# First phase of one diffusion-transformer layer on one core: the context's transfers as one piece behind the first two tiles, and a tile's products always behind the next tile's modulation

## The chip, the cores and the metric

The kernel runs on one core of a Trainium2 chip, with TensorE (PE, weight loads shown apart as PEld), VectorE (DVE), ScalarE (ACT), GpSimd (POOL) and SyncE (SP, which here issues nearly all transfers). The metric is the device time of one execution in microseconds; lower is better.

## The reference, cut to what matters

One layer over 256 latent tokens `x` and 256 context tokens `ctx`, D_MODEL = 2048, all in float32:

```python
mod   = (jax.nn.silu(c)     @ w_mod[l] + b_mod[l])[:, None, :]
sa, ca, ga, sm, cm, gm = jnp.split(mod, 6, axis=-1)
mod_c = jax.nn.silu(c_ctx)  @ w_mod[l] + b_mod[l]
...
h_c = modulate(x_ctx, norm_attn_w[l], sa_c, ca_c)     # rmsnorm(x) * (1 + scale) + shift
p_c_kv = h_c @ w_in[l][:, K_OFF:P_OFF]                # keys and values of the context
h = modulate(x, norm_attn_w[l], sa, ca)
p = h @ w_in[l]                                       # queries, keys, values, pool input, gates
...
mix = token_mixer(...)                                # attention + pooling, gated
x = x + ga * mix
x = x + gm * sq_relu_mlp(modulate(x, norm_mlp_w[l], sm, cm), w_ff1[l], w_ff2[l])
```

The change lies in the first phase: the shift `sa` and scale `ca` of both token sets, the hidden states `h` and `h_c` made from them, and the first half (512 columns, "group 0") of the queries of `x` and of the keys of `x` and `ctx`.

## The kernel before, in words

**Tiles.** D_MODEL is cut into 16 tiles `f` of 128 features (`KT = 16`). For each tile the kernel loads four 512 KB pieces of the modulation weight (`w_m`, f, i = 0..3), and PE multiplies them with the two conditioning vectors into a PSUM bank (`mod_tile`; 32 recorded matmuls a tile, rows `mod<-raw,cv`). ACT copies the result out (`rows`), PE turns it into columns (`modT`), ACT copies these (`col`), DVE adds bias and norm weight (`col`, L378 and L379). Then `hidden(f, t, ...)` makes the tile's modulated tokens, for x (t = 0, `hL`) and for the context (t = 1, `hC`): DVE `hw`, ACT the high part, DVE the low part. Every float32 product is made of three matmuls of parts (`mm3`): high by high, high by low, low by high.

**Products.** The weights of queries and keys come in pieces of two tiles (`w_q` and `w_k`, group 0, pair j for the tiles 2j and 2j+1). `load_next` issues the transfer and then splits the piece: ACT casts the high part (L224) and DVE subtracts the low part (L225). For each tile PE then runs 18 matmuls of 512 columns: two token tiles times three matmuls for each of "kx" (keys of x), "q" (queries) and "kc" (keys of the context). The high part's matmul of a token tile comes first, the low part's second.

**Order of transfers.** `plan` writes out the stream of pieces by hand, and SP issues them in this order; a piece waits in SP's queue until its buffer is free. The plain pieces (`raw`) share 5 buffers: the four `w_m` pieces of an even tile, and each `w_k` and `w_q` piece. The pieces of an odd tile have four buffers of their own. Context tokens (`cT`, four transfers of 512 KB) stand between `w_m` pieces of tiles 2 and 3. Pieces j = 0, 1, 3, 4, .. 7 stand behind the odd tile f = 2j+1, and piece 2 behind tile 6.

**Order on PE.** It is fixed by hand in this phase (`ordered_pe`). In the loop over `f`, `PACE[f]` steps of a list of products (`order`, a step is three matmuls) are put around the turn of tile f: half before `mod_columns`, half behind. The list lags: at odd tile f it works on a pair whose pieces were split a tile or more before, and the last 12 steps (pair 7) stand behind the loop. Context squares are summed at tiles 2 and 3, the context's scale `rms` is made at tile 4, and the context's hidden states of tiles 0 to 6 follow at tiles 4, 5 and 6 (`context`).

**Order on ACT and DVE at an odd tile.** Behind the tile's `mod` matmuls ACT has `rows`, the cast of the keys' piece (`first`), then `col` and the cast of the queries' piece (`whi`), and DVE the matching subtractions. The lines that set this are

```python
for w in ("w_k", "w_q"):
    held[w, j] = wchunk(w, 0, j, ahead=FIRST_AHEAD if j < 7 else 1)
steps(PACE[f] // 2)
cols[f] = mod_columns(f, rows)
```

After the phase come values, attention beside pooling and gates, the output projection and the MLP; nothing of these is edited.

Of the kernel before, what the change touches and what calls it, by code (L numbers as in the profile page):

```python
# [19 lines left out]
KT = D // P  # L20
# [28 lines left out]
def layer(ctx: ExitStack, tc, a, out):  # L49
# [21 lines left out]
    def bank(name):  # L71
        return psum.tile([P, 512], F32, tag="ps", name=name)

    def work(name, shape=None, dt=F32):
        return pool.tile(shape or [P, 512], dt, tag="w2", name=name, bufs=9)

    def s16(name, shape, dt=F32):
        return pool.tile(shape, dt, tag="s16", name=name, bufs=7)
# [4 lines left out]
    def small(name, n):  # L83
        return pool.tile([P, 16], F32, tag="sm", name=name, bufs=12)[:, 0:n]
# [14 lines left out]
    def tick():  # L99
        for w in waiting:  # L100
            w[0] -= 1
        while waiting:
            due = [w for w in waiting if w[0] <= 0]
            if not due:
                break
            waiting.remove(due[0])
            due[0][1]()
# [10 lines left out]
    def chain(*gens):  # L118
        for g in gens:
            yield from g  # L120
# [5 lines left out]
    def plan(name, *idx, rate=0.0):  # L126
        stream.append(((name,) + idx, rate))
# [3 lines left out]
    for f in range(KT):  # L131
        for i in range(4):
            plan("w_m", f, i)
            if f in (2, 3) and i % 2 == 1:
                plan("cT", 2 * f - 4 + i // 2)
            if (f, i) == (9, 0):
                plan("prq")
        j = 2 if f == 6 else -1 if f == 5 or f % 2 == 0 else f // 2
        if j >= 0:
            plan("w_k", 0, j)  # L140
            plan("w_q", 0, j)
    for n, g, rate in (("w_v", 0, 1.5), ("w_q", 1, 1.0), ("w_k", 1, 1.5), ("w_v", 1, 1.5)):
        for ch in range(8):
            plan(n, g, ch, rate=rate)
# [27 lines left out]
    FIRST_AHEAD = 3  # L172
# [22 lines left out]
    def load_next():  # L195
        key, rate = stream[len(loaded)]
        src = a[key[0]]
        for i in key[1:]:
            src = src[i]
        if key[0] == "prq":  # L200
            nc.sync.dma_start(prq, src)
            loaded.append((key, None, None))
            return
        if key[0] in ("cT", "x"):
            dst = cT[:, 4 * key[1]:4 * key[1] + 4, :] if key[0] == "cT" else x1_tile()[:, key[1], key[2] * 512:key[2] * 512 + 512]
            nc.sync.dma_start(dst, src)
            loaded.append((key, None, None))
            return
        n = src.shape[-1]
        if key[0] == "w_m":  # L210
            raw = mod_raw(*key[1:])
            sp.dma_start(raw, src)
            loaded.append((key, raw, raw))
            return
        raw = raw_chunk(src, n)
        if key[:2] == ("w_k", 0):
            if not first:
                first.append(s16("first", [P, 4, 1024], F32R))
            i = 2 * (key[2] % 2)
            hi, lo = first[0][:, i, :], first[0][:, i + 1, :]  # L220
        else:
            hi = pool.tile([P, n], F32R, tag="whi", name="whi", bufs=3)
            lo = pool.tile([P, n], F32R, tag="wlo", name="wlo", bufs=3)
        act.copy(hi, raw)  # L224
        vec.tensor_sub(lo, raw, hi.bitcast(F32))  # L225
        loaded.append((key, hi, lo))
        credit[0] += rate
        credit_rate[0] = rate
        while credit[0] >= 1.0:
            credit[0] -= 1.0  # L230
            if late[0] is not None:
                next(late[0], None)

    def wchunk(*key, ahead=AHEAD):
        while len(loaded) < min(done[0] + 1 + ahead, len(stream)) or loaded[done[0]][1] is None:
            if loaded and done[0] < len(loaded) and loaded[done[0]][1] is None:
                done[0] += 1
                continue
            load_next()
        got, hi, lo = loaded[done[0]]  # L240
        assert got == key, (got, key)
        loaded[done[0]] = None
        done[0] += 1
        tick()
        return hi, lo
# [27 lines left out]
    cT = s16("cT", [P, KT, T])  # L273
# [3 lines left out]
    def pr(name):  # L277
        lo, hi = PRM[name]
        return prm[:, lo:hi]
# [89 lines left out]
    def mod_columns(f, rows):  # L369

        pt = bank("modT")
        for a in range(2):
            pe.matmul(pt[:, 2 * a:2 * a + 2], rows[:, a * P:a * P + P], quads, start=a == 0, stop=a == 1,
                      skip_group_check=True)
        col = small("col", 4)
        act.copy(col, pt[:, 0:4])
        c3 = col.rearrange("p (a c) -> p a c", a=2)
        vec.tensor_add(c3, c3, bias2[:, :, f:f + 1].broadcast_to([P, 2, 2]))  # L378
        vec.tensor_scalar(c3[:, 0, :], c3[:, 0, :], pr("nw")[:, f:f + 1], None, ALU.mult)  # L379
        return c3  # L380

    def hidden(f, t, c3):

        src, h = ((xT, hL), (cT, hC))[t]
        u = work("hw", [P, T])
        ht, k8 = h[f // 8], f % 8
        bias = c3[:, 1, t:t + 1]
        vec.scalar_tensor_tensor(u, src[:, f, :], c3[:, 0, t:t + 1], rms[t], ALU.mult, ALU.mult)
        act.activation(ht[:, 0, k8, :], u, AF.Identity, bias=bias)
        vec.scalar_tensor_tensor(ht[:, 1, k8, :], u, bias, ht[:, 0, k8, :].bitcast(F32), ALU.add, ALU.subtract)  # L390

    def tokens(nt):
        return [(hL, 0), (hL, 1), (hC, 0), (hC, 1)][:nt]

    def xmm(banks, toks, k, hi, lo, sl, first, last):
        for ps, (h, t) in zip(banks, toks):
            mm3(ps, tok(h, k, 0, t), tok(h, k, 1, t), hi[:, sl], lo[:, sl], first, last)
# [72 lines left out]
    fb = {}  # L470
    held = {}

    def pair_steps(n, j):

        w = "w_q" if n == "q" else "w_k"
        if w not in fb:
            fb[w] = [bank(f"{w}_{t}") for t in range(4 if n != "q" else 2)]
        hi, lo = held[w, j]
        for kk in range(2):
            k = 2 * j + kk  # L480
            for t in range(2):
                t4 = t + (2 if n == "kc" else 0)
                xmm([fb[w][t4]], [tokens(4)[t4]], k, hi, lo, slice(kk * 512, kk * 512 + 512), k == 0, k == KT - 1)
                yield

    def steps(n):
        for _ in range(n):
            next(side, None)

    order = [("kx", 0), ("q", 0), ("kx", 1), ("q", 1), ("kc", 0), ("kc", 1), ("kx", 2), ("q", 2), ("kc", 2)]  # L490
    for j in range(3, 7):
        order += [("kx", j), ("q", j), ("kc", j)]
    side = chain(*(pair_steps(*o) for o in order))
    PACE = (0, 0, 4, 4, 6, 6, 8, 8) + (6,) * 8

    cols = {}
    total = []

    def context_squares(i):

        sq = [work("sq") for _ in range(2)]
        for h in range(2):
            act.activation(sq[h], cT[:, 4 * i + 2 * h:4 * i + 2 * h + 2, :].rearrange("p a t -> p (a t)"), AF.Square)
        vec.tensor_add(sq[0], sq[0], sq[1])
        if total:
            vec.tensor_add(total[0], total[0], sq[0])
        else:
            total.append(sq[0])


    context = {4: (0, 1), 5: (2, 3, 4), 6: (5, 6)}
    ordered_pe[0] = True
    sb = bank("ssq")
    for i in range(4):
# [2 lines left out]
    for f in range(KT):  # L517
        if f % 2 == 0:
            ps = bank("mod")
        rows = mod_tile(f, ps)  # L520
        if f == 4:
            sq = total[0]
            vec.tensor_add(sq[:, 0:T], sq[:, 0:T], sq[:, T:2 * T])
            sb = bank("ssq")
            pe.matmul(sb[:, 0:T], mean, sq[:, 0:T], start=True, stop=True)
            rms.append(rsq(sb[:, 0:T], T, P / D, "rms"))
        j = 2 if f == 6 else -1 if f == 5 or f % 2 == 0 else f // 2
        if j >= 0:
            for w in ("w_k", "w_q"):
                held[w, j] = wchunk(w, 0, j, ahead=FIRST_AHEAD if j < 7 else 1)  # L530
        steps(PACE[f] // 2)
        cols[f] = mod_columns(f, rows)
        steps(PACE[f] - PACE[f] // 2)
        hidden(f, 0, cols[f])
        for k in context.get(f, (f,) if f > 6 else ()):
            hidden(k, 1, cols[k])
        if f in (2, 3):
            for i in range(2):
                context_squares(2 * f - 4 + i)
        if f == 10:  # L540
            tables()
    lasts = [pair_steps(n, 7) for n in ("kx", "q", "kc")]
    for _ in range(2):
        for g in lasts:
            next(g)
            next(g)
    ordered_pe[0] = False
    kb, qb = fb["w_k"], fb["w_q"]
    qT = s8("qT", [P, NH, T])
# [558 lines left out]
```

## Time and profile before

| | us |
|---|---|
| median of 3 runs (1491.62 to 1492.20) | 1492.11 |
| the profiled execution: its own time | 1492.22 |
| its span, first to last instruction | 1490.40 |
| around the span (time less span) | 1.82 |
| first phase: first `mod` matmul to the first matmul of the values | 12.63 to 143.35 |
| `mod` matmuls of tile 5 start | 54.60 |
| `mod` matmuls of tile 15 start | 128.66 |

The profiled execution lies 0.11 us above the median. In a timeline row the first two numbers are start and length in us, `xN` the recorded instructions merged into the row, and a bracket at its end is the idle time of the engine before it and what ended it. A row of stages gives, after the two limits, its length and then the busy time and the count of each engine, the granted PE clock (1.00 is full), the busy share of the DMA engines and GB/s.

### The profile page before, as it was taken

The numbers are of one execution on the slowest core, as the hardware profiler recorded it, in microseconds if no ns is written. First come the engines' busy times: TensorE is split into PE (matmuls) and PEld (weight loads), VectorE is DVE, ScalarE is ACT, GpSimd is POOL, SyncE is SP. The second block draws the span as 40 slices with busy tenths as digits, with TensorE's granted clock in tenths as the row PEclk, the third lists the DMA queues.
The fourth block names the chain that finished last, engine by engine and source line by source line (L and its number), as shares of the span: only waits on it lengthen the run. The fifth ranks groups of instructions, "written<-read, shape, count | busy, mean of one in ns | idle before, by whom it ended". The sixth has DMA issues, their size and how long they took to land.

```text
span 1490.4 us, 19996 instructions
## 1 busy us (share of the span) xinstructions
PE 1450.0 (97%) x7578; PEld 1201.2 (81%) x7578; DVE 992.8 (67%) x1220; ACT 694.3 (47%) x956; POOL 121.2 (8%) x120
## 2 busy tenths in 40 slices
PE   5899999999899999999989999999999999999998
PEld 3567887778788888888879888888888888888887
DVE  3555988859887676767675765666666555555675
ACT  4435344555554444445444654545445453544532
POOL 0000101101410000000000100100000000000260
PEclk8999999999999999999999999999999999999999
DMA  9898696556678887897746777677776656666664
GB/s 380 314 371 309 206 313 215 156 162 205 212 247 269 267 269 260 263 311 257 230 147 201 239 238 238 223 234 237 242 235 215 192 190 193 188 192 190 186 197 140
DMA packets 97440, 347.85 MB, mean 233 GB/s; under 512 B 11072, under 2 KB 11712, under 8 KB 97344
## 3 DMA queue, kind: packets, MB, share of 16 engines
q1 hardware_dynamic: 96768, 345.50, 70.5%
q8 instruction: 59, 0.97, 0.3%
q0 software_dynamic: 576, 1.08, 0.2%
q14 instruction: 37, 0.30, 0.1%
HBM read 344.44 MB, written 2.10 MB: 233 GB/s over the span
## 4 chain that ended last, share of the span: by engine, by line
PE 90%; DMA 4%; DVE 3%; ACT 1%; issue 1%; SPq 1%; POOL 0%; DVEq 0%; POOLq 0%; ACTq 0%
PE f L957 14%; PE f L418 8%; PE f L419 8%; PE f L421 8%; PE f L960 7%; PE pg L419 4%; PE pg L418 4%; PE pg L421 4%; DMA raw<-in_w_m_dram 2%; PE wo L419 2%; PE wo L418 2%; PE wo L421 2%; PE pyy L418 2%; PE pyy L419 2%; PE pyy L421 2%; PE w_k L67 2%
## 5 line engine op out<-in xcount | busy, mean ns | idle before, releaser
L225 DVE TENSOR_TENSOR wlo<-raw,whi 128x1024 fp32r<-128x1024 f32 x443 | 547.6, 1238 | 355.5 <-ACT whi L224 334.3
L224 ACT CAST whi<-raw 128x1024 fp32r<-128x1024 f32 x443 | 463.8, 1048 | 577.0 <-PE f L419 184.8
L957 PE MATMUL f<-h,whi 128*128 128x512 f32 x896 | 224.2, 392 | 0.0
L418 PE MATMUL f<-whi,act 128*128 128x512 f32 x512 | 199.3, 389 | 0.0
L419 PE MATMUL f<-whi,act 128*128 128x512 f32 x512 | 199.3, 389 | 0.0
L957 PEld LDWEIGHTS f<-h,whi 128*128 128x128 f32 x896 | 161.7, 189 | 29.3
L598 DVE SCALAR_TENSOR_TENSOR macc<-raw,sil,macc 128x1024 f32<-128x1024 f32 x128 | 167.8, 1311 | 2.3 <-DMA macc<-in_b_ga_dram 1.3
L421 PE MATMUL f<-wlo,act 128*128 128x512 f32 x512 | 136.8, 389 | 0.0
L960 PEld LDWEIGHTS f<-h,wlo 128*128 128x128 f32 x896 | 122.2, 190 | 8.7
L960 PE MATMUL f<-h,wlo 128*128 128x256 f32 x896 | 124.9, 282 | 0.0
L421 PEld LDWEIGHTS f<-wlo,act 128*128 128x128 f32 x512 | 96.1, 188 | 19.9
L418 PEld LDWEIGHTS f<-whi,act 128*128 128x128 f32 x512 | 96.2, 188 | 19.8
L419 PEld LDWEIGHTS f<-whi,act 128*128 128x128 f32 x512 | 96.1, 188 | 19.8
L418 PE MATMUL pg<-whi,hL 128*128 128x512 f32 x256 | 100.7, 394 | 0.0
L419 PE MATMUL pg<-whi,hL 128*128 128x512 f32 x256 | 99.7, 389 | 0.0
L968 POOL TENSOR_TENSOR rsq<-relu 128x512 f32<-128x512 f32 x28 | 29.1, 1041 | 537.2 <-ACT relu L967 516.9
L421 PE MATMUL pg<-wlo,hL 128*128 128x512 f32 x256 | 68.5, 389 | 0.0
L419 PEld LDWEIGHTS pg<-whi,hL 128*128 128x128 f32 x256 | 48.1, 188 | 10.2 <-issue 0.2
L418 PEld LDWEIGHTS pg<-whi,hL 128*128 128x128 f32 x256 | 48.1, 188 | 10.2 <-ACT whi L224 0.2
L421 PEld LDWEIGHTS pg<-wlo,hL 128*128 128x128 f32 x256 | 48.1, 188 | 10.0
L67 PE MATMUL mod<-raw,cv 128*32 128x256 f32 x512 | 36.5, 401 | 15.6 <-DMA raw<-in_w_m_dram 15.6
L418 PE MATMUL wo<-whi,mix 128*128 128x512 f32 x128 | 49.9, 390 | 0.0
(254 smaller groups left out, 2116.9 us busy)
## 6 DMA issues: line engine op xcount, KB each, us to landing
raw<-in_w_ff_dram SPq DMA_DIRECT2D x240, 512.0 KB, 4.3
raw<-in_w_m_dram SPq DMA_DIRECT2D x64, 512.0 KB, 8.3
raw<-in_w_ga_dram SPq DMA_DIRECT2D x32, 512.0 KB, 4.5
raw<-in_w_cm_dram SPq DMA_DIRECT2D x32, 512.0 KB, 4.5
raw<-in_w_gb_in_dram SPq DMA_DIRECT2D x32, 512.0 KB, 4.5
raw<-in_w_ga_in_dram SPq DMA_DIRECT2D x32, 512.0 KB, 4.7
raw<-in_w_sm_dram SPq DMA_DIRECT2D x32, 512.0 KB, 5.0
raw<-in_w_o_dram SPq DMA_DIRECT2D x32, 512.0 KB, 4.5
```

The costliest lines, as they stand in the source:

```text
L67: return (lambda *a, **k: pin(emit(*a, **k))) if self.flag[0] else emit
L224: act.copy(hi, raw)
L225: vec.tensor_sub(lo, raw, hi.bitcast(F32))
L418: pe.matmul(banks[t], tok(h, k, 0, tt), wt, start=k == 0, stop=False)
L419: pe.matmul(banks[t], tok(h, k, 1, tt), wt, start=False, stop=False)
L421: pe.matmul(banks[t], tok(h, k, 0, tt), wt, start=False, stop=k == 2 * nk - 1)
L598: pin(vec.scalar_tensor_tensor(acc, raw, sil[:, 0, k:k + 1], acc, ALU.mult, ALU.add))
L957: pe.matmul(ps, hi[:, kk * P:kk * P + P], both(h2, k), start=k == 0, stop=False)
L960: pe.matmul(ps[:, T:2 * T], lo[:, kk * P:kk * P + P], act_slice(h2, k, 0), start=False, stop=k == KT - 1)
L968: gp.tensor_mul(sq, r, r)
```

## The change

The plan now puts the `w_k` and `w_q` piece j behind each odd tile f = 2j+1, piece 2 too, and the four context transfers behind the first such pair. The list of steps and `PACE` are gone: `products(n, k)` runs one tile's six matmuls of one kind. At tile 1, products "kx" and "q" of tiles 0 and 1 follow, then the squares, sum and scale of the whole context, and the context's hidden states of tiles 0 and 1. At tile 2, "kc" of tiles 0 and 1. From tile 3 on, behind the `mod` matmuls of tile f: "kx" of tile f-1, the turn and both hidden states of tile f, "q" and "kc" of tile f-1. Tile 15's own 18 matmuls stand behind the loop.

```diff
@@ plan
-            if f in (2, 3) and i % 2 == 1:
-                plan("cT", 2 * f - 4 + i // 2)
...
-        j = 2 if f == 6 else -1 if f == 5 or f % 2 == 0 else f // 2
-        if j >= 0:
-            plan("w_k", 0, j)
-            plan("w_q", 0, j)
+        if f % 2 == 1:
+            plan("w_k", 0, f // 2)
+            plan("w_q", 0, f // 2)
+        if f == 1:
+            for i in range(4):
+                plan("cT", i)
@@ products
-    order = [("kx", 0), ("q", 0), ("kx", 1), ("q", 1), ("kc", 0), ("kc", 1), ("kx", 2), ("q", 2), ("kc", 2)]
...
-    PACE = (0, 0, 4, 4, 6, 6, 8, 8) + (6,) * 8
+    def products(n, k):
+        w = "w_q" if n == "q" else "w_k"
...
+        hi, lo = held[w, k // 2]
+        c = (k % 2) * 512
+        for t in range(2):
+            t4 = t + (2 if n == "kc" else 0)
+            xmm([fb[w][t4]], [tokens(4)[t4]], k, hi, lo, slice(c, c + 512), k == 0, k == KT - 1)
+    def modulate(f, rows):
+        cols[f] = mod_columns(f, rows)
+        hidden(f, 0, cols[f])
+        if f > 1:
+            hidden(f, 1, cols[f])
@@ loop over f, behind rows = mod_tile(f, ps)
-        if f == 4:
+        if f < 3:
+            modulate(f, rows)
+        if f % 2 == 1:
+            for w in ("w_k", "w_q"):
+                held[w, f // 2] = wchunk(w, 0, f // 2, ahead=5 if f == 1 else FIRST_AHEAD if f < KT - 1 else 1)
+        if f == 1:
+            for k in range(2):
+                products("kx", k)
+                products("q", k)
+            for i in range(4):
+                context_squares(i)
             sq = total[0]
...
+            for k in range(2):
+                hidden(k, 1, cols[k])
+        elif f == 2:
+            products("kc", 0)
+            products("kc", 1)
+        elif f > 2:
+            products("kx", f - 1)
+            modulate(f, rows)
+            products("q", f - 1)
+            products("kc", f - 1)
...
+    for n in ("kx", "q", "kc"):
+        products(n, KT - 1)
```

On SP, before, from the first modulation pieces on (`xN` merges equal rows): one context transfer after every second `w_m` piece of tiles 2 and 3.

```order
L212 DMA raw<-in_w_m_dram 128x1024 x8
L115 DMA raw<-in_w_k_dram 128x1024
L115 DMA raw<-in_w_q_dram 128x1024
L212 DMA raw<-in_w_m_dram 128x1024 x2
L206 DMA cT<-in_cT_dram 128x1024
L212 DMA raw<-in_w_m_dram 128x1024 x2
L206 DMA cT<-in_cT_dram 128x1024
L212 DMA raw<-in_w_m_dram 128x1024 x2
L206 DMA cT<-in_cT_dram 128x1024
L212 DMA raw<-in_w_m_dram 128x1024 x2
L206 DMA cT<-in_cT_dram 128x1024
```

On SP now, at the same place:

```order
L212 DMA raw<-in_w_m_dram 128x1024 x8
L115 DMA raw<-in_w_k_dram 128x1024
L115 DMA raw<-in_w_q_dram 128x1024
L212 DMA raw<-in_w_m_dram 128x1024
L206 DMA cT<-in_cT_dram 128x1024 x4
L212 DMA raw<-in_w_m_dram 128x1024 x7
L115 DMA raw<-in_w_k_dram 128x1024
L115 DMA raw<-in_w_q_dram 128x1024
```

All four context transfers moved ahead of the second `w_m` piece of tile 2.

On PE, before, at tiles 1 to 3 (`w_k_249` and `w_k_250` are the banks of the keys of x, one for each token tile):

```order
L67 MATMUL mod<-raw,cv 32x256 x16
L67 MATMUL modT<-prm,rows 128x2 x2
L67 MATMUL mod<-raw,cv 32x256 x16
L67 MATMUL w_k_249<-first,hL_92 128x512 x3
L67 MATMUL w_k_250<-first,hL_92 128x512 x3
L67 MATMUL modT<-prm,rows 128x2 x2
L67 MATMUL w_k_249<-first,hL_92 128x512 x3
L67 MATMUL w_k_250<-first,hL_92 128x512 x3
L67 MATMUL mod<-raw,cv 32x256 x16
```

On PE now, the end of what stands between the `mod` matmuls of tiles 1 and 2 and what follows (the banks are now 223 and 224 for the keys of x, 225 and 226 for the context's keys, 233 and 234 for the queries):

```order
L67 MATMUL w_q_233<-whi,hL_92 128x512
L67 MATMUL w_q_234<-whi,hL_92 128x512
L67 MATMUL w_q_234<-wlo,hL_92 128x512
L67 MATMUL w_q_234<-whi,hL_92 128x512
L67 MATMUL ssq<-sq,mean 128x256
L67 MATMUL mod<-raw,cv 32x256 x16
L67 MATMUL modT<-prm,rows 128x2 x2
L67 MATMUL w_k_225<-first,hC_94 128x512 x3
L67 MATMUL w_k_226<-first,hC_94 128x512 x3
```

24 products of tiles 0 and 1 and the context's sum (`ssq`) moved ahead of tile 2's `mod` matmuls, and the context's keys directly behind its turn.

On PE, before, at an odd tile (13); `w_q_327` and `w_q_328` are the banks of the queries, 251 and 252 those of the context's keys:

```order
L67 MATMUL mod<-raw,cv 32x256 x16
L67 MATMUL w_q_327<-whi,hL_93 128x512
L67 MATMUL w_q_327<-wlo,hL_93 128x512
L67 MATMUL w_q_327<-whi,hL_93 128x512
L67 MATMUL w_q_328<-whi,hL_93 128x512
L67 MATMUL w_q_328<-wlo,hL_93 128x512
L67 MATMUL w_q_328<-whi,hL_93 128x512
L67 MATMUL w_k_251<-first,hC_95 128x512 x3
L67 MATMUL modT<-prm,rows 128x2 x2
L67 MATMUL w_k_252<-first,hC_95 128x512 x3
L67 MATMUL w_k_251<-first,hC_95 128x512 x3
L67 MATMUL w_k_252<-first,hC_95 128x512 x3
```

On PE now, at the same tile:

```order
L67 MATMUL mod<-raw,cv 32x256 x16
L67 MATMUL w_k_223<-first,hL_93 128x512 x3
L67 MATMUL w_k_224<-first,hL_93 128x512 x3
L67 MATMUL modT<-prm,rows 128x2 x2
L67 MATMUL w_q_233<-whi,hL_93 128x512
L67 MATMUL w_q_233<-wlo,hL_93 128x512
L67 MATMUL w_q_233<-whi,hL_93 128x512
L67 MATMUL w_q_234<-whi,hL_93 128x512
L67 MATMUL w_q_234<-wlo,hL_93 128x512
L67 MATMUL w_q_234<-whi,hL_93 128x512
L67 MATMUL w_k_225<-first,hC_95 128x512 x3
L67 MATMUL w_k_226<-first,hC_95 128x512 x3
```

Before, the 18 matmuls behind tile 13's `mod` were those of the pair 5, whose pieces were split two tiles earlier; now they are those of tile 12, with piece 6 (`first`, `whi`), which is split behind the same `mod` matmuls.

More of the change, by code (lines that the diff above doesn't have):

```diff
@@ L471, in layer @@
     held = {}
-    def pair_steps(n, j):
+    def products(n, k):
         w = "w_q" if n == "q" else "w_k"
@@ L477, in pair_steps @@
             fb[w] = [bank(f"{w}_{t}") for t in range(4 if n != "q" else 2)]
[L478 to L488, printed above, removed]
-    order = [("kx", 0), ("q", 0), ("kx", 1), ("q", 1), ("kc", 0), ("kc", 1), ("kx", 2), ("q", 2), ("kc", 2)]
-    for j in range(3, 7):
-        order += [("kx", j), ("q", j), ("kc", j)]
-    side = chain(*(pair_steps(*o) for o in order))
-    PACE = (0, 0, 4, 4, 6, 6, 8, 8) + (6,) * 8
+        hi, lo = held[w, k // 2]
[3 more added lines that the diff above has]
+            xmm([fb[w][t4]], [tokens(4)[t4]], k, hi, lo, slice(c, c + 512), k == 0, k == KT - 1)
     cols = {}
@@ L508, in context_squares @@
             total.append(sq[0])
-    context = {4: (0, 1), 5: (2, 3, 4), 6: (5, 6)}
+    def modulate(f, rows):
[3 more added lines that the diff above has]
+            hidden(f, 1, cols[f])
     ordered_pe[0] = True
@@ L526, in layer @@
             rms.append(rsq(sb[:, 0:T], T, P / D, "rms"))
[L527 to L539, printed above, removed]
+            for k in range(2):
[8 more added lines that the diff above has]
+            products("kc", f - 1)
         if f == 10:
             tables()
[L542 to L546, printed above, removed]
+    for n in ("kx", "q", "kc"):
+        products(n, KT - 1)
     ordered_pe[0] = False
```

## The prediction

> **What bounds the kernel now.** I read the page's slices of the span first, then busy times by stage, then PE's timeline with its waits, then ACT and DVE around one odd tile. The page's clock row: only the second slice is cold.
>
> ```profile
> PEclk8999999999999999999999999999999999999999
> ```
>
> The stages (first phase in three parts, then the values):
>
> ```profile
> core 0: us, PE busy (x) PEld busy (x) DVE busy (x) ACT busy (x) POOL busy (x), PEclk, DMA share, GB/s
> 12.63:54.60 41.97, 29.11 (x225) 15.68 (x224) 19.46 (x40) 15.47 (x33) 0.00 (x0) 0.84 0.98 384
> 54.60:128.66 74.06, 70.32 (x553) 48.31 (x553) 38.45 (x97) 26.35 (x56) 0.00 (x0) 1.00 0.91 345
> 128.66:143.35 14.69, 14.69 (x92) 11.62 (x91) 8.09 (x13) 8.64 (x16) 0.00 (x0) 1.00 0.87 317
> 143.35:280.00 136.65, 136.65 (x621) 108.60 (x620) 119.76 (x189) 63.90 (x117) 17.45 (x10) 1.00 0.67 220
> ```
>
> Up to tile 5 (54.60) the transfers bound: share 0.98, PE idle 12.9 of 42 us and the clock at 0.84. From tile 5 to tile 15 PE is idle only 3.7 of 74 us, and never afterwards. So the early waits are what can be won, and a new PE wait behind tile 5 is paid in full. PE's rows there (tiles 13 to 15, and the last matmuls of the phase):
>
> ```profile
> 114.56 1.93 PE L67 MATMUL mod<-raw,cv 128*32 128x256 f32 x32
> 116.42 0.50 PE L67 MATMUL w_q<-whi,hL 128*128 128x512 f32 x1
> 116.76 0.40 PE L67 MATMUL w_q<-wlo,hL 128*128 128x512 f32 x1
> 118.96 2.29 PE L67 MATMUL w_k<-first,hC 128*128 128x512 f32 x9
> 121.18 1.51 PE L67 MATMUL mod<-raw,cv 128*32 128x256 f32 x24
> 123.33 0.64 PE L67 MATMUL mod<-raw,cv 128*32 128x256 f32 x8 [0.64 <-DMA raw<-in_w_m_dram]
> 128.66 1.93 PE L67 MATMUL mod<-raw,cv 128*32 128x256 f32 x32
> 135.19 1.52 PE L67 MATMUL w_k<-first,hL 128*128 128x512 f32 x6
> 136.55 0.39 PE L67 MATMUL w_q<-whi,hL 128*128 128x512 f32 x1
> 143.35 0.39 PE L418 MATMUL v<-whi,hL 128*128 128x512 f32 x1
> ```
>
> A tile without a wait lasts 121.18 - 114.56 = 6.62 us (32 `mod`, the turn, 18 products). Six products last 136.55 - 135.19 = 1.36, one 0.227, eighteen 4.09. The waits left are for the last piece of an even tile, 0.64 us here. Five pairs of tiles take 74.06 us, 14.8 each, against 13.24 without waits.
>
> **The odd tile, now in series.** The same tile 13 on ACT and DVE:
>
> ```profile
> 116.56 0.37 ACT L366 COPY rows<-mod 128x256 f32<-128x256 f32 x1 [1.90 <-PE mod L67]
> 116.83 1.05 ACT L224 CAST first<-raw 128x1024 fp32r<-128x1024 f32 x1
> 117.91 1.23 DVE L225 TENSOR_TENSOR first<-raw,first 128x1024 fp32r<-128x1024 f32 x1 [2.74 <-ACT first L224]
> 119.19 1.05 ACT L224 CAST whi<-raw 128x1024 fp32r<-128x1024 f32 x1
> ```
>
> The keys' piece was there already (no wait for a transfer); its cast starts behind `rows`, which waits for the tile's own `mod`. Its low part is ready at 117.91 + 1.23 = 119.14. Before, nobody needs it for another tile. Now "kx" of the tile before is the next work on PE and needs exactly this piece: its first matmul only the high part, its second the low part. At tile 13 the second could run at 116.76 and gets its operand at about 119.19 (0.05 for the signal): PE stands 2.43 us. Queued behind it on PE are the turn, "q" and "kc", and so `col`, both hidden states and the next `mod`. The queries' piece is cast 1.05 us behind the keys', its low part 1.23 behind the keys' low part, at about 120.4; "q" comes only at 119.2 + 1.14 + 0.36 = 120.7 and waits for nothing. This holds at tiles 5, 7, .. 15: six stalls of s = 2.43 us. At tile 3 the cast stands ahead of `rows` on ACT, so only part of it is left (below).
>
> **The even tile's wait goes.** Its last piece takes the buffer of the keys' piece, free when the low part is made:
>
> ```profile
> 119.17 4.12 DMA raw<-in_w_m_dram
> ```
>
> That is issue to landing, so 7 us behind the odd tile's `mod`. With the stall, the next tile's fourth piece is used 2.43 + 4.76 + 1.4 = 8.6 us behind it (4.76 = 121.18 - 116.42; 1.4 for three pieces, 1.86 a tile): covered by 1.6 us. If that cover goes, the 0.64 comes back at each pair.
>
> **The early part, up to the start of tile 5's `mod`.** Bound by transfers and by the context's chain; the rows are
>
> ```profile
> 19.47 0.64 PE L67 MATMUL mod<-raw,cv 128*32 128x256 f32 x8 [0.65 <-DMA raw<-in_w_m_dram]
> 23.30 1.08 PE L67 MATMUL mod<-raw,cv 128*32 128x256 f32 x8 [2.09 <-DMA raw<-in_w_m_dram]
> 24.02 1.23 DVE L225 TENSOR_TENSOR wlo<-raw,whi 128x1024 fp32r<-128x1024 f32 x1
> L503 ACT ACTIVATE sq<-cT 128x512 f32<-128x512 f32 x8 | 4.7, 622 | 0.0
> L504 DVE TENSOR_TENSOR sq<-sq 128x512 f32<-128x512 f32 x4 | 2.8, 688 | 0.4 <-ACT sq L503 0.3
> 47.84 0.67 PE L67 MATMUL ssq<-sq,mean 128*128 128x256 f32 x2
> 50.51 0.42 DVE L265 SCALAR_TENSOR_TENSOR rms<-rq_t,rms 128x256 f32<-128x256 f32 x1
> ```
>
> Up to 20 us nothing differs. Tile 2's first piece lands at 23.30; one transfer is 524 KB at 411 GB/s (the row of the clock, below), 1.28 us. Four context transfers land by 28.4, the rest of tile 2 by 32.2 (before, one context piece lay in between). Meanwhile PE runs the 24 products of tiles 0 and 1: from 23.7, when the keys' low part is there (the queries' is at 25.25), at half clock up to 28.15, some ten products of 0.454, then the other 13 at 0.227, to about 31.2. (The clock's windows are shown below; the one from 24.74 is now busy.) Squares (two of 0.62), DVE's sums (0.69, 0.69, 0.43) put `ssq` at 31.5. Tile 2's `mod` then ends at 33.9; the scale takes 50.93 - 47.84 = 3.1 and the context's `hw` and `hC` about 1.5 more, and tile 2's `rows` stands behind them on ACT: "kc" of tiles 0 and 1 starts at 36.6, 2.7 us idle. 12 products end at 39.4, tile 3's `mod` at 41.4, "kx" of tile 2 runs, "q" waits about 1.3 for the queries' piece (cast behind tile 3's `rows`), "kc" ends at 46.7; one tile of 6.62 brings tile 5 to 53.4, 1.2 earlier than 54.60. Bounds: 21 transfers behind 23.3 allow no earlier than 48.8; with the clock half for one more window it would be 56.1.
>
> **Sum at full clock.** Start of tile 5: -1.2. Five pairs: 5 x (13.24 + 2.43) = 78.4 against 74.06, +4.3. From tile 15's `mod` to the values: 6.62 + 2.43 + 4.09 = 13.1 against 14.69, -1.6 (six products fewer are left). Together +1.5, or -13.0 + 6s. Removed at no gain: the 12 products behind the loop only change place. The phase behind (PE 136.65 of 136.65) shifts as a whole.
>
> **The clock.** Windows on the grid on which the clock moved:
>
> ```profile
> 17.91:21.32 3.41, 1.88 (x20) 0.84 (x20) 0.48 (x1) 0.48 (x4) 0.00 (x0) 1.00 1.03 411
> 21.32:24.74 3.42, 1.24 (x12) 0.36 (x16) 3.14 (x6) 2.47 (x4) 0.00 (x0) 0.50 1.03 410
> 28.15:31.56 3.41, 3.21 (x19) 1.33 (x16) 0.00 (x0) 0.37 (x1) 0.00 (x0) 0.50 1.03 410
> 31.56:34.97 3.41, 3.41 (x30) 2.43 (x29) 1.11 (x4) 1.47 (x4) 0.00 (x0) 1.00 1.03 410
> 41.80:45.21 3.41, 1.89 (x24) 0.50 (x24) 2.96 (x4) 3.02 (x5) 0.00 (x0) 1.00 0.51 144
> 45.21:48.62 3.41, 1.41 (x16) 0.88 (x13) 2.41 (x5) 0.45 (x2) 0.00 (x0) 1.00 0.97 364
> 48.62:52.04 3.42, 3.42 (x11) 2.65 (x9) 1.27 (x3) 0.91 (x2) 0.00 (x0) 0.50 1.02 406
> 52.04:55.45 3.41, 3.41 (x30) 2.44 (x32) 2.67 (x8) 1.47 (x4) 0.00 (x0) 1.00 1.01 408
> 48.16 3.98 PE L67 MATMUL w_k<-first,hL 128*128 128x512 f32 x9
> ```
>
> A window of 3.41 us with PE busy 1.88 or 1.41 was followed by one at half clock; one with 1.89 was not; a busy one brings the clock back. Nine products took 3.98 us there against 2.29: a half-clock window costs 1.7. In a stall PE's rows would be idle 1.4 us (116.49, the end of `mod`, to 117.93, the end of the cast and the signal), busy 0.39, idle 0.9 (to 119.19). A window that holds 1.53 us of this idle time goes cold by the first row: the position allows 0.7 + 2 x 0.77 = 2.25 of 3.41, 66%; by the 1.41 row 38%. A pair of 15.7 us shifts against the grid by 2 us, so six stalls meet most positions: between 2 and 4 windows. I take 4, since the 1.88 row went cold too: +6.8. Ends: none, and six (+10.2).
>
> The Trainium skill ("TensorE: Matmul & The Clock Gate", "HAM oscillation — how this bites in real kernels") warns only of PE gaps above about 3.4 us; by it no stall here would cool the clock, and the sum would stay at +1.5. The trace speaks against it: the longest gap before 48.62 was 2.0 us.
>
> **Sum.** 1492.2 + 1.5 + 6.8 = 1500.5 (the profiled execution's own time is 1492.22, the median 1492.11: no difference that matters).
>
> **The rivals.**
> 1. *Stalls, but the clock stays full* (one window at most): +1.5 to +3.2, 1493.7 to 1495.4. For it: 41.80 with 1.89 stayed warm. Against: a full stall leaves about 1.1 busy, less than 1.41.
> 2. *Faster: the weight split does not hold PE.* If the low part were ready when "kx" begins, pairs last 13.24 and the sum is -13.0: 1479.2. It decides at s = 2.2 us: below this, with a warm clock, the early gain outweighs the stalls. For it: transfers would allow it (ten in 12.8 us a pair). Against: `rows` 0.37, cast 1.05, subtraction 1.23 stand in one chain, in the rows above.
> 3. *The even tile's last piece stays late as well*: 0.64 to 1.3 more at each of five pairs, on top of the forecast: 1503.7 to 1507. Against: the cover of 1.6 us.
> 4. *The change moves nothing*: early gain of up to 5.8 (tile 5 at 48.8) against the stalls, near 1492. Against: the context's chain holds tile 2.
>
> **How the numbers follow.** About 0.2% (3 us) can be told from no change. Forecast (two to six cold windows) 0.60; rival 1 0.16, nearly all within 0.2%; rival 2 0.09, faster; rival 3 0.10, slower; rival 4 0.05. So slower 0.72, same 0.19, faster 0.09. The range leaves out rival 2 and the far end of 3: 1493 to 1507.
>
> **What would show it.** In the profile after, PE waits at tiles 5, 7, .. 15 for DVE's `first`, 0.9 to 1.2 us, behind a wait for ACT's `first` of 1.2 to 1.5; no waits for `w_m` pieces behind tile 5; pairs of 15.7 us or more; `mod` of tile 5 at 53.4; windows of 0.50 behind several odd tiles. It is wrong if the low part is there earlier, if the clock stays 1.00, or if tile 5 starts outside 49 to 56.

## The result

The kernel now takes 1506.07 us (median of 4 runs, 1504.59 to 1507.11); the kernel before, beside it, 1492.15 (4 runs, 1491.62 to 1495.04). The ratio is 1.0093 (95% 1.0081 to 1.0105): slower by 0.9%. The forecast was 1500.5 (1493 to 1507). The profiled execution after took 1506.7 us with a span of 1504.9 us; the spans differ by 14.5 us. Every number below is of profiled executions where no median is named.

The same three stretches of the first phase and an equally long one behind it, in the profile after (columns as before: busy time of each engine, granted clock, DMA share):

```profile
12.52:56.43 43.91, 35.68 (x256) 22.41 (x255) 23.35 (x48) 17.54 (x36) 0.00 (x0) 0.88 0.99 383
56.43:141.78 85.35, 74.34 (x541) 51.83 (x540) 35.57 (x89) 24.09 (x51) 0.00 (x0) 0.92 0.81 305
141.78:156.54 14.76, 12.56 (x74) 9.51 (x73) 7.38 (x11) 7.07 (x12) 0.00 (x0) 0.88 0.69 241
156.54:293.19 136.65, 136.31 (x620) 108.23 (x619) 119.25 (x189) 64.90 (x120) 17.47 (x10) 1.00 0.67 220
```

The limits are the start of tile 0's `mod`, of tile 5's, of tile 15's, and the first phase's end (only values follow from 157.90 on; six matmuls of the values, 1.36 us, now stand ahead of that and are counted out). Against 41.97, 74.06 and 14.69 before: +1.9, +11.3 and +0.1, which is 13.3. The last matmul of the program starts 13.36 us later than before (1497.93 against 1484.57), so the phases behind only shift. The other 1.1 us lie behind the last matmul, where the output is stored. From the start of that matmul to the end of the span it is 5.8 us before and 7.0 after, and between 5.6 and 6.7 in the eight profiles of the experiments; single executions differ by as much there, so this part is not put down to the change.

In the middle stretch the transfers went from share 0.91 to 0.81 and the clock from 1.00 to 0.92: PE no longer waits for weights there (the four waits for `raw` that are left stand at tiles 0 and 1), but for their split. PE's waits in the first phase, before and then after (total us, times, longest):

```profile
PE mod L67 <- DMA raw<-in_w_m_dram: 15.6, 20, 2.3
PE modT L67 <- ACT rows L366: 1.0, 2, 0.5
```

```profile
PE w_k L67 <- ACT first L224: 9.8, 7, 1.4
PE w_k L67 <- DVE first L225: 5.3, 7, 0.8
PE modT L67 <- ACT rows L366: 3.5, 3, 2.5
PE mod L67 <- DMA raw<-in_w_m_dram: 1.4, 4, 0.6
PE ssq L67 <- DVE sq L527: 1.0, 1, 1.0
PE w_q L67 <- DVE wlo L225: 0.4, 1, 0.4
```

**An odd tile, after.** PE, ACT and DVE at tile 5; a bracket holds the idle time before a row and what ended it:

```profile
56.43 1.93 PE L67 MATMUL mod<-raw,cv 128*32 128x256 f32 x32
59.80 0.49 PE L67 MATMUL w_k<-first,hL 128*128 128x512 f32 x1 [1.44 <-ACT first L224]
61.06 1.95 PE L67 MATMUL w_k<-first,hL 128*128 128x512 f32 x5 [0.77 <-DVE first L225]
58.43 0.37 ACT L366 COPY rows<-mod 128x256 f32<-128x256 f32 x1 [2.58 <-PE mod L67]
58.70 1.05 ACT L224 CAST first<-raw 128x1024 fp32r<-128x1024 f32 x1
59.78 1.22 DVE L225 TENSOR_TENSOR first<-raw,first 128x1024 fp32r<-128x1024 f32 x1 [3.41 <-ACT first L224]
```

`rows` cannot start before tile 5's own `mod` has ended, the cast follows `rows`, the subtraction follows the cast, and "kx" of tile 4 needs both. Its second matmul could have run at 59.80 - 1.44 + 0.23 = 58.59 and ran at 61.06: 2.47 us, against s = 2.43. Such a pair of waits stands at tile 1 and at tiles 5, 7, .. 15 (seven in the list of waits).

**The clock.** Windows on the grid of this execution, 3.41 us each; the last three columns are the clock, the DMA share and GB/s, the first busy time is PE's:

```profile
13.97:17.38 3.41, 2.02 (x28) 0.98 (x28) 1.57 (x6) 0.53 (x2) 0.00 (x0) 1.00 1.03 410
17.38:20.80 3.42, 2.96 (x24) 0.41 (x18) 0.77 (x2) 0.51 (x1) 0.00 (x0) 0.50 1.02 407
34.45:37.87 3.42, 0.95 (x16) 0.47 (x8) 2.80 (x7) 1.16 (x3) 0.00 (x0) 0.99 1.03 410
37.87:41.28 3.41, 3.41 (x10) 2.73 (x11) 2.15 (x6) 2.00 (x4) 0.00 (x0) 0.50 1.02 408
58.35:61.76 3.41, 1.21 (x6) 0.81 (x5) 1.98 (x2) 2.26 (x3) 0.00 (x0) 1.00 0.09 35
61.76:65.17 3.41, 3.41 (x12) 2.83 (x11) 1.59 (x5) 0.41 (x2) 0.00 (x0) 0.50 0.87 300
92.48:95.89 3.41, 1.21 (x18) 0.34 (x6) 1.30 (x2) 2.26 (x3) 0.00 (x0) 1.00 0.45 178
95.89:99.31 3.42, 3.42 (x10) 2.96 (x11) 1.12 (x2) 0.16 (x1) 0.00 (x0) 0.50 0.73 222
99.31:102.72 3.41, 3.41 (x9) 2.64 (x9) 2.10 (x6) 0.91 (x2) 0.00 (x0) 0.50 1.02 362
112.96:116.37 3.41, 2.04 (x10) 1.52 (x10) 2.36 (x2) 1.50 (x2) 0.00 (x0) 1.00 0.22 34
126.61:130.03 3.42, 1.79 (x25) 0.71 (x17) 0.71 (x1) 2.06 (x3) 0.00 (x0) 1.00 0.81 321
147.09:150.51 3.42, 3.42 (x12) 2.84 (x11) 2.73 (x6) 1.33 (x3) 0.00 (x0) 0.51 0.81 250
```

A stall that falls into one window leaves PE busy 1.21 us there, and the next window runs at half clock (tiles 5, 7, 9 and 15; behind tile 9 two in a row). A stall that a window's edge divides (tiles 11 and 13: 2.04 and 1.79 busy) costs no clock. So `mod` of the odd tiles starts at 56.43, 73.83, 91.24, 110.19, 125.97 and 141.78: pairs of 17.40, 17.41, 18.95, 15.78 and 15.81 us. The pairs without a cold window (a window at half clock) are close to the forecast's 15.67; each cold window adds 1.6.

### The profile page after: what moved, and what is told of

Its sections match the earlier page's. It is cut to its first block, busy times and chain, and to the rows that moved or that the text cites. A ratio compares the mean times of both kernels' runs of the same rounds, so it can differ in the third digit from the quotient of the medians.

```text
span 1504.9 us, 19996 instructions
## 1 busy us (share of the span) xinstructions
PE 1458.4 (97%) x7578; PEld 1208.6 (80%) x7578; DVE 992.5 (66%) x1220; ACT 693.8 (46%) x956; POOL 121.5 (8%) x120
## 4 chain that ended last, share of the span: by engine, by line
PE 90%; DVE 4%; DMA 2%; ACT 2%; POOL 1%; issue 1%; SPq 0%; DVEq 0%; POOLq 0%; ACTq 0%
PE f L955 14%; PE f L419 8%; PE f L418 8%; PE f L421 8%; PE f L958 7%; PE pg L418 4%; PE pg L419 4%; PE pg L421 4%; PE w_k L67 3%; PE pyy L418 2%; PE wo L419 2%; PE wo L418 2%; PE wo L421 2%; PE pyy L419 2%; PE pyy L421 2%; PE mod L67 2%
## 5 line engine op out<-in xcount | busy, mean ns | idle before, releaser
L418 PE MATMUL wo<-whi,mix 128*128 128x512 f32 x128 | 49.9, 390 | 0.0
L419 PE MATMUL wo<-whi,mix 128*128 128x512 f32 x128 | 49.8, 389 | 0.0
```

What stands on the lines that cost most here:

```text
L418: pe.matmul(banks[t], tok(h, k, 0, tt), wt, start=k == 0, stop=False)
L419: pe.matmul(banks[t], tok(h, k, 1, tt), wt, start=False, stop=False)
```

## The experiments

Two theories stood after the result. **A, the split:** the odd tile's chain (`rows`, cast, subtraction) holds PE 2.4 us at each odd tile, and these gaps cool the clock. **B, the transfers:** the phase is bound by what the transfers deliver or by the context's chain; the stalls only sit where PE would have waited anyway, and come back as waits for weights when they are taken away. E1 to e4 ran with 18 runs of the kernel before (1492.05 median), e5 to e8 with 13 (1490.85).

### e1: both weight pieces behind the even tile

```diff
@@ the plan, and the same in the loop over f
-        if f % 2 == 1:
+        if f % 2 == 0:
             plan("w_k", 0, f // 2)
             plan("w_q", 0, f // 2)
```

How many pieces `wchunk` reads ahead follows the new plan.

> The changed kernel, with the key and query pieces of a pair loaded behind its even tile instead of its odd tile; order on PE as in the change. If the loss is the weight split in series with PE: the six stalls of 2.43 us go (14.6 us), and with them the five half-clock windows behind tiles 5, 7, 9 and 15 (8.5 us): 1506 - 23 = 1483 us, between 1480 and 1489, and PE waits for no split. If the stalls only stand where waits for modulation pieces would otherwise be (buffers and transfers bind): most of it comes back as waits for w_m, about 1500 us.

1504.12 us (4 runs), ratio 1.0079 (1.0059 to 1.0100), where theory A gave 1483. By its time alone it speaks for B. The waits of PE and of SP (the latter from 50 to 150 us), SP's rows, and then PE's:

```profile
PE mod L67 <- DMA raw<-in_w_m_dram: 16.5, 22, 2.5
```

```profile
SPq L115 <- PE mod L67: 30.6, 6, 7.5
```

```profile
111.33 0.33 SPq L115 DMA_DIRECT2D raw<-in_w_k_dram  x1
120.77 0.33 SPq L115 DMA_DIRECT2D raw<-in_w_q_dram  x1
121.19 4.09 SPq L212 DMA_DIRECT2D raw<-in_w_m_dram  x8
```

```profile
113.42 0.64 PE L67 MATMUL mod<-raw,cv 128*32 128x256 f32 x8 [0.65 <-DMA raw<-in_w_m_dram]
114.71 0.64 PE L67 MATMUL mod<-raw,cv 128*32 128x256 f32 x8 [0.64 <-DMA raw<-in_w_m_dram]
```

The waits for the split are gone, as A says. But of five `raw` buffers the even tile's four modulation pieces and the keys' piece take all; the queries' piece needs the buffer of a modulation piece of the very same tile. SP issues in order: it stood from 111.7 to 120.8 before the queries' piece, and eight modulation pieces, four of them the next odd tile's with buffers of their own, stood behind it. This repeats at each pair; PE's two rows are from the odd tile whose pieces came out behind such a hold one pair earlier (its last three pieces each come late). PE's 16.5 us are those of the whole phase; behind tile 5 they are 12.0, where the change had none, against 13.3 for the six stalls. Behind the waits at tile 7 two windows run at half clock (79.5 to 86.3; 0.96 on average from tile 5 to tile 15). So e1 took one wait away and made another, and decides nothing between A and B. I had costed the move without walking SP's queue.

### e2: the gap filled, the stall left

```diff
         elif f > 2:
+            if f % 2 == 1 and f > 3:
+                for _ in range(18):
+                    pe.matmul(ps[:, 0:T], tok(hL, 0, 0, 0), act_slice(hL, 0, 0), start=True, stop=True)
             products("kx", f - 1)
```

> The changed kernel with 18 extra matmuls of 256 columns (about 2.1 us) on PE in each of the six stalls; they write a half of the modulation bank that has been read, and no result uses them. If the stalls cool the clock: the stalls stay, 15.7 us a pair, the clock is 1.00 from tile 5 on, and the five windows' 8.5 us go: 1497.5 us, between 1496 and 1500. If gaps of this length do not cool the clock, or the low clock has another cause: no change, 1506 us or a little more.

1498.28 us (8 runs), ratio 1.0043 (1.0030 to 1.0055). PE at tile 9, and the stretch from tile 5 to tile 15:

```profile
90.80 2.40 PE L67 MATMUL mod<-hL 128*128 128x256 f32 x18 [0.49 <-ACT rows L366]
93.04 1.55 PE L67 MATMUL w_k<-first,hL 128*128 128x512 f32 x6
```

```profile
56.49:136.19 79.70, 77.25 (x631) 57.59 (x630) 35.63 (x89) 24.14 (x51) 0.00 (x0) 1.00 0.85 326
```

The extra matmuls cover most of the stall and end slightly behind it: pairs are 15.94 us each instead of 15.8. The clock is 1.00 throughout, and the stretch is 85.35 - 79.70 = 5.65 us shorter although PE does more. With the cold window at tile 15, that is about what five cold windows (8.5 us) less six times 0.14 give, 7.7; the medians differ by 7.8, the ratios by 0.5% or 7.5 us. Shown: the half-clock windows are made by the idle time in the stall, and cost some 8 us. B has no place for this gain, since no transfer was changed.

### e3: only the context in one piece, in the kernel before

```diff
-            if f in (2, 3) and i % 2 == 1:
-                plan("cT", 2 * f - 4 + i // 2)
...
+        if f == 1:
+            for i in range(4):
+                plan("cT", i)
```

> The kernel before, with only the four context transfers moved behind the first pair of key and query pieces; all orders on PE as before. If the loss is the split behind the odd tile: three transfers of 1.28 us are ahead of tile 2's pieces, given back by tile 3; 1492 to 1495.5 us. If the context's piece is what costs: 1500 us or more.

1492.48 us (10 runs), ratio 1.0002 (0.9992 to 1.0011): no change. Tile 2's `mod` waits once for 5.3 us, and gets it back later. By itself the context's place costs nothing; the loss lies in the order of the products, or needs it.

### e4: products two tiles behind

```diff
-        elif f > 2:
-            products("kx", f - 1)
+        elif f == 3:
             modulate(f, rows)
-            products("q", f - 1)
-            products("kc", f - 1)
+        elif f > 3:
+            products("kx", f - 2)
+            modulate(f, rows)
+            products("q", f - 2)
+            products("kc", f - 2)
...
-    for n in ("kx", "q", "kc"):
-        products(n, KT - 1)
+    for k in (KT - 2, KT - 1):
+        for n in ("kx", "q", "kc"):
+            products(n, k)
```

> The changed kernel with the products of a tile two tiles behind its modulation instead of one, transfers as in the change; 36 products behind the loop instead of 18. If the series of split and product is the loss: no wait for the split, clock 1.00 from tile 5 on, 1483 to 1488 us. If it is the place of the pieces in the stream of transfers: still above 1500 us.

1488.30 us (5 runs), ratio 0.9967 (0.9953 to 0.9981): 1.2% less than the change by the ratios, and below the kernel before (0.3 us above the range that A gave). The stretch from tile 5 to tile 15, and PE's waits:

```profile
53.47:124.71 71.24, 67.89 (x542) 46.06 (x541) 35.13 (x89) 24.98 (x51) 0.00 (x0) 1.00 0.97 371
```

```profile
PE mod L67 <- DMA raw<-in_w_m_dram: 4.8, 10, 0.7
PE modT L67 <- ACT rows L366: 4.5, 5, 2.5
```

No odd tile waits for the split (one wait is left, at tile 1), the clock is full, and a pair takes 14.25 us; the stretch is 14.1 us shorter than in the change. That settles A: the change's order costs what the distance of one tile to the split costs. It is also the first bound for B: without stalls, waits for weights come up, 3.3 us of the 4.8 behind tile 5, a quarter of the 13.3 us that the six stalls took.

### e6 and e5: the context's sum later, in the change and in e4

The context's `ssq`, its scale and the context's hidden states of tiles 0 and 1 behind tile 2's `mod`, and "kc" of tiles 0 and 1 behind tile 3's, meant to close the 2.47 us gap at tile 2:

```diff
         if f < 3:
-            modulate(f, rows)
+            cols[f] = mod_columns(f, rows)
+            hidden(f, 0, cols[f])
...
+        elif f == 2:
             sq = total[0]
...
-            for k in range(2):
+            for k in range(3):
                 hidden(k, 1, cols[k])
-        elif f == 2:
+        if f == 3:
             products("kc", 0)
             products("kc", 1)
```

> The changed kernel, with the context's sum, scale and hidden states behind tile 2's modulation and the context's keys of tiles 0 and 1 behind tile 3's; transfers and the odd tiles as in the change. If the early part is lost to the context's chain (PE's wait of 1.0 us for the sum, 2.5 for rows behind hC on ACT, and the half-clock window that follows): 2 to 5 us less, 1501 to 1504 us, and tile 5 starts at 51.5 to 54.5 instead of 56.4. If the early part is bound by transfers: 1505.5 to 1507 us.

> Products two tiles behind (as in e4, 1488.3 us) together with the later context sum of e6. If both costs are separate and add: 2 to 4 us below e4, 1484 to 1486.5 us. If transfers bind from tile 5 on in e4: no gain, 1488 us.

e6: 1504.27 us (4 runs), ratio 1.0095 (1.0081 to 1.0109), beside 1.0093 for the change. e5: 1487.86 us (8 runs), ratio 0.9974 (0.9963 to 0.9985), beside 0.9967 for e4. Neither gained; the expected starts of tile 5 in e6 (51.5 to 54.5) were missed by its 57.09. The wait of 2.5 us is gone (longest for `rows` 0.5), but e6's PE meets the transfers instead:

```profile
38.13 0.64 PE L67 MATMUL mod<-raw,cv 128*32 128x256 f32 x8 [0.57 <-DMA raw<-in_w_m_dram]
39.40 0.64 PE L67 MATMUL mod<-raw,cv 128*32 128x256 f32 x8 [0.63 <-DMA raw<-in_w_m_dram]
41.26 4.68 PE L67 MATMUL w_k<-first,hC 128*128 128x512 f32 x12 [1.22 <-ACT hC L389]
```

Tile 3's `mod` now follows tile 2's so closely that it waits for its own pieces, the context's hidden states come 1.22 us late, and the 12 context products meet a half-clock window again (4.68 us). Tile 0 also started 2.2 us later in e6's profile than in that of the change; from tile 0 to tile 5 it is 42.38 against 43.91, a gain of 1.5 that its median doesn't show. So up to tile 5 a repair of the chain alone is worth nothing measurable: as B says, part of the gap comes back as waits for transfers, and the rest as a wait for the context and a half-clock window. That the transfers alone bound this part is not shown.

### e7: only the keys' piece behind the even tile

```diff
@@ the plan
-        if f % 2 == 1:
+        if f % 2 == 0:
             plan("w_k", 0, f // 2)
+        else:
             plan("w_q", 0, f // 2)
@@ loop over f
-        if f % 2 == 1:
-            for w in ("w_k", "w_q"):
-                held[w, f // 2] = wchunk(w, 0, f // 2, ahead=...)
+        w = "w_q" if f % 2 else "w_k"
+        held[w, f // 2] = wchunk(w, 0, f // 2, ahead=...)
```

> The changed kernel, with only the key piece of a pair behind its even tile; the query piece stays behind the odd tile, so that the odd tile's modulation pieces do not queue on SP behind a piece that waits for its buffer (what held e1). If the stall is the split of whichever piece is used first: the keys' stall of 2.43 us becomes a wait for the queries' low part of 0.7 to 0.8 us, too short to cool the clock: 1506 - 6 x 1.7 - 8.5 = 1487.5 us, between 1485 and 1491. If the SP queue holds the pieces again: above 1495 us.

1484.71 us (4 runs), ratio 0.9961 (0.9947 to 0.9975), 0.3 us below the range that the first case gave: by the ratios 1.3% less than the change, and 1.2% (some 17 us) less than e1, by where the queries' piece stands. PE's waits and the stretch from tile 5 to tile 15:

```profile
PE w_q L67 <- DVE wlo L226: 3.6, 7, 0.8
PE modT L67 <- ACT rows L367: 3.5, 3, 2.5
PE mod L67 <- DMA raw<-in_w_m_dram: 2.2, 5, 0.8
```

```profile
57.14:128.33 71.19, 68.01 (x542) 46.83 (x541) 35.14 (x90) 24.23 (x51) 0.00 (x0) 1.00 0.97 376
```

The keys' piece takes the fifth buffer and holds up nothing; only the queries' split is still behind the odd tile's `mod`, under "kx", and 0.4 to 0.8 us of it show. All five waits for modulation pieces stand at tiles 0 and 1. The order of products is the change's own, one tile behind. So the order is not bad by itself: with the keys split a tile earlier it beats the kernel before.

### e8: e7, with the context's sum later and the queries last

e7 with the edit of e6, and in the loop

```diff
             products("kx", f - 1)
             modulate(f, rows)
-            products("q", f - 1)
             products("kc", f - 1)
+            products("q", f - 1)
```

> The key piece early as in e7, the context's sum later as in e6, and at each tile the context's keys ahead of the queries, so that the queries' split has 1.36 us more. If the three costs are separate: no wait for a split, 4 us below e7 for the queries and 2 to 4 for the context, 1478 to 1483 us. If the transfers bind first: 1484 to 1488 us.

1481.10 us (5 runs), ratio 0.9935 (0.9922 to 0.9949): the best version, 0.65% below the kernel before and 1.6% below the change. The stretch and all of PE's waits in the first phase:

```profile
56.39:124.55 68.16, 67.03 (x542) 46.38 (x541) 34.88 (x89) 24.53 (x51) 0.00 (x0) 1.00 0.96 373
```

```profile
PE mod L67 <- DMA raw<-in_w_m_dram: 5.4, 11, 0.7
PE modT L67 <- ACT rows L367: 1.5, 3, 0.5
```

A pair takes 13.63 us, close to the 13.24 without waits. Which of the two added edits brought how much of the 3.6 us beyond e7 was not tried apart; the stretch alone, where the queries' place acts, is 3.0 us shorter. The split's waits are gone as expected, but three separate costs would have given 6 to 8 us, so their adding up is not shown.

## Why the prediction was right, and where its terms were off

The likeliest case came: stalls at the odd tiles and half-clock windows behind them. The size was too small, +8.3 forecast against +13.9 by the medians, and 1506.07 lies only 0.9 us inside the upper end of the range; that the range held it is in part luck. Step by step:

- **The stall, s = 2.43 us at six odd tiles:** 2.47 measured at tile 5, the waits 1.44 and 0.77 where 1.2 to 1.5 and 0.9 to 1.2 were named (the second is a little below). Pairs without a cold window are 15.8 against 15.67. e4 and e7 show that it is the split: one takes the products further from it, the other the split further from the products, and both lose the stalls.
- **The even tile's wait of 0.64:** gone; from tile 5 on no `raw` wait appears (1.4 us in the whole phase, against 15.6). Rival 3 did not come, though its time of 1503.7 to 1507 did, from other terms.
- **The cold windows:** four were forecast for +6.8; there were five from tile 5 on (two behind tile 9) for about 8.5 at the forecast's price of 1.7, 8.0 at the measured 1.6, and e2's 7.8 agrees. Five instead of four is the first of the two terms that were too small, by 1.7. Four of the six stalls cooled the clock, the number that was taken; the fifth window is the second one behind tile 9, which the forecast didn't have. Rival 1, stalls with a full clock, did not come. The rule of the Trainium skill ("TensorE: Matmul & The Clock Gate", "HAM oscillation — how this bites in real kernels"), no PE gaps above about 3.4 us, would have let these stalls pass. The trace does not agree: the longest gap in the phase was 2.47 us, those of a stall 1.44 and 0.77, and the clock halved behind four of six stalls. (The kernel before had a gap of 2.32 us too, ahead of 27.99, longer than the 2.0 that the prediction names.)
- **The early part, the step that failed:** tile 5 was to start at 53.4 (-1.2) and started at 56.43 (+1.8), 0.4 outside the bounds of 49 to 56, so by its own sign the prediction was wrong here. The rows there, ACT's last squares of the context and then PE's:

```profile
29.32 1.15 ACT L491 ACTIVATE sq<-cT 128x512 f32<-128x512 f32 x2 [0.20 <-DMA cT<-in_cT_dram]
32.44 0.70 PE L67 MATMUL ssq<-sq,mean 128*128 128x256 f32 x2 [1.04 <-DVE sq L527]
33.07 1.93 PE L67 MATMUL mod<-raw,cv 128*32 128x256 f32 x32
37.47 0.71 PE L67 MATMUL modT<-prm,rows 128*128 128x2 f32 x4 [2.47 <-ACT rows L366]
38.03 4.48 PE L67 MATMUL w_k<-first,hC 128*128 128x512 f32 x12
42.44 1.93 PE L67 MATMUL mod<-raw,cv 128*32 128x256 f32 x32
```

  The last context transfer let ACT start at 29.32, where 28.4 was forecast; the squares and DVE's sums behind it took their time as forecast, and `ssq` came at 32.44 instead of 31.5. The gap at tile 2 was forecast nearly right (2.7; 2.47 measured), but what it does was left out: it left PE busy 0.95 us of its window (34.45 above), the next one ran at half clock, and the 12 context products took 4.4 us (38.03 to 42.44) instead of 2.8. I applied the clock's rule to the stalls and not to the gap that I had worked out myself; "one more window" stood there only as the bound of 56.1 (55.1 by the forecast's own price of 1.7). This term is off by 3.0 us, the largest error: 0.9 from the later context, 1.6 from the half clock, and some 0.5 between `ssq` and the products. No run took that half-clock window away, so its share is read from the rows alone.
- **Rivals 2 and 4:** the start gained nothing of rival 4's 5.8 us (whose 48.8 is 20 transfers of 1.28 us behind 23.3; the 21 that it names give 50.2). Rival 2's condition, the low part ready when "kx" begins, was set up by e4 and e7: 1488.3 and 1484.7 us, faster than before as it said, though not 1479. In e4 waits for transfers behind tile 5 (3.3 us) take part of it, in e7 those for the queries' low part (3.6 us in the phase) and the start of tile 5, which stayed late (57.14).
- **The queries' wait of about 1.3 us at tile 3:** 0.44 in PE's row. **The tail:** 14.76 us; 13.1 with one window's 1.7 is 14.8. (It lost 18 matmuls, 74 recorded against 92, where the forecast says six products; its sum has the 18.)

Together: forecast +8.3 for the profile; the early part 3.0 more, a window more 1.7, and 1.1 at the program's end, which is not put down to the change: 14.1, against 14.5 measured by spans.

What stays open: why the clock stayed at half for a second window behind tile 9 (95.89 to 99.31 was fully busy), what bounds the part up to tile 5 once the context's sum is later, and how the gain of e8 over e7 divides between its two edits.

## What to carry to other kernels

Before products are moved closer to their operands, follow the operand's whole preparation (copy, cast, subtraction) on its engines: here a distance of one tile put three short instructions behind the tile's own matmuls, and 2.4 us of PE at every second tile. Price such a gap with what it does to the clock in the next window too, at every gap in the forecast, and not only at those that repeat. And before a transfer is moved earlier, ask which buffer it takes and what stands behind it in the issuing queue: with both pieces moved (e1) the kernel was no better, with one (e7) 1.3% faster than the change.

## What was not expected of the hardware

- Short gaps cool the clock. Windows of 3.41 us in which PE was busy 0.95 or 1.21 us were followed by one at half clock; windows with 1.79 and 2.04 were not. But the kernel before has 1.88 followed by a cold one, and the changed one has 2.02 (13.97 to 17.38, above), so recorded busy time alone doesn't decide near 1.8 to 2.0.
- A window fully busy at half clock did not always bring the clock back (95.89 to 99.31, then 0.50 once more; the same in e6 from 79.22 to 86.05).
- A transfer that waits for its buffer holds all transfers behind it on SP, those with free buffers too: 30.6 us of SP's waits in e1 between 50 and 150 us, and 12.0 us of PE's behind tile 5, where e7, with the queries' piece a tile later, has none.
